# Partial sums of a layer's first two chunks in five stretches instead of two, their weight loads placed by the modulation's progress

## The chip, the cores and the metric

The kernel runs on one core of one Trainium2 chip. The metric is the device time of one execution in microseconds; the median of a few runs counts.

## The reference

The reference is a two-layer diffusion backbone. Each layer modulates its normalised input, projects it through one wide matrix, and runs two token mixers on the parts (differential attention and a gated MLP) before an output projection. What matters here is how a layer begins:

```python
mod = silu_c @ w_ada[layer] + b_ada[layer]                 # 2048 -> 3 x 2048
shift, scale, gate = [m[:, None, :] for m in jnp.split(mod, 3, axis=-1)]
hn = _rmsnorm(h, norm_g) * (1.0 + scale) + shift           # 256 latent + 256 context tokens
z = hn @ w_in                                              # 2048 -> 11264
q, k, v, ga, ub, vb, gb, mg = jnp.split(z, cuts, axis=-1)
```

Each feature of `hn` needs its own columns of `w_ada`, and each column of `z` contracts over all 2048 features, 16 tiles of 128. All is float32; the kernel splits every operand of the large products into a high and a low float32r part and multiplies three times (high by high, high by low, low by high).

## The kernel before

Every engine gets its instructions in the order in which a planner (`Builder`) writes them. The planner keeps an estimate of the time on each engine and interleaves a stream of weight products on PE with side work written as generators. What it writes is fixed in the built program: at run time each engine goes through its list in order and waits on semaphores.

**Pieces.** Weights come from memory in pieces of 512 KB in the order of a list, `plan`. SP issues all their loads, in that order, into four buffers named `raw`. There are two kinds. A piece of `w_in` holds two feature tiles by 512 columns; ACT casts it into `wh`, DVE subtracts to get `wl` (line 47 is the helper through which all work on DVE, ACT and POOL is issued), and then its `raw` buffer is free. A piece of `w_ada` for layer 0 holds four feature tiles by 256 columns (`ada4_segs`) and is read by PE as it lies in `raw`; its buffer is free when PE has used it. Below, A1 to A64 are these 64 pieces of layer 0's modulation in order; on PE each is four matmuls `ms<-raw,s` (eight in the profile, two passes each).

**Modulation.** Layer 0's shift and scale are made in eight groups of two feature tiles; a group is eight pieces, four for the shift and four for the scale (`ada_pe`). After each four, ACT copies the row and PE turns it into columns (`ms<-c,w`, the column matmuls); after eight, `x_trans` transposes the two feature tiles of the tokens (`ms<-c,s`, four per tile), DVE applies scale and shift, and ACT and DVE split the result into the operand `x`. So feature tiles 2g and 2g+1 can be multiplied only after group g.

**The first two chunks.** X (queries and keys of the first pair of heads) and Y (the first 512 columns of v) are products of 512 tokens by 512 columns over the 16 feature tiles. A *step* is one token tile by one feature tile: three matmuls of 512 columns, `mm<-wh,x`, `mm<-wl,x`, `mm<-wh,x`. A piece of `w_in` makes eight steps, both chunks 128. There are four PSUM banks `mm`, as many as one chunk has token tiles. X's first half (tiles 0 to 7) is accumulated, copied by ACT into an SBUF tile (`keep`), then Y's first half, then the second halves, whose sums DVE adds to the parked ones (`drop`, `from_psum`). A table `quota` says how many steps stand before each modulation piece: none before the first 14, one before each of the next 26, two before each of the last 24, 74 in all; the remaining 54 follow. The pieces of `w_in` stand in the plan one place ahead of A14, A22, A30, A38, A43 and so on. The look-ahead of the loads (`loads`) is six pieces, as far as `raw` buffers are free.

Of the kernel before, what the change touches and what calls it, by code (L numbers as in the profile page):

```python
# [38 lines left out]
class Engine:  # L39
    """An engine whose instructions run in the order in which they are written."""  # L40

# [12 lines left out]
class Builder:  # L54
    """Interleaves the stream of weight matmuls with everything else. Side work is written as
    generators; a yield waits for what the generator has issued and may ask for buffers."""

# [25 lines left out]

# [1 line left out]
    def t(self, tag, shape, dt=F32):  # L85
# [19 lines left out]

# [1 line left out]
    def account(self, key, name, kw):  # L107
# [35 lines left out]

# [1 line left out]
    def spawn(self, gen, urgent=False, front=False):  # L145
# [33 lines left out]
    def loads(self):  # L179
        while self.nraw < min(self.at + 6, len(self.plan)) and len(self.pool["raw"]) > self.spare:  # L180
            self.grab("raw", 1, 1e18)
            i = self.nraw
            self.nraw += 1
            if i in self.extra:
                self.extra[i]()
            self.ready[i] = Event()
            self.spawn(self.split(i), urgent=True)
# [34 lines left out]

# [1 line left out]
    def matmul(self, out, lhsT, rhs, start, stop, slow=1.0):  # L224
# [20 lines left out]

# [1 line left out]
    def hl(self, h, l, src):  # L247
# [15 lines left out]

# [1 line left out]
    def load(self, segs, kt):  # L265
# [29 lines left out]
    def piece(self, segs, kt):  # L295
# [6 lines left out]
        return self.ready.pop(i).hl  # L302

    def piece_done(self, tag="wh"):
        self.pool[tag].append(self.now)

    def tok_steps(self, ps, xh, xl, segs, tiles, k0, k1, nk=KT, first=0, on_tile=None, pre=None, front=False):
        """out[tokens of a tile, columns] += x[tokens, k] w[k, columns]"""
        for kt in range(k0, k1, 2):
            if pre is not None:  # L310
                pre(kt)
            h, l = self.piece(segs, kt)
            for t, c0, c1 in tiles:
                if t not in ps:
                    self.take("mm")
                    ps[t] = self.bank("mm")
                for k in range(2):
                    ts = slice(t * P, (t + 1) * P)
                    self.mm3(ps[t][:, c0:c1], xh(kt + k)[:, ts], xl(kt + k)[:, ts],
                             h[:, k, c0:c1], l[:, k, c0:c1], kt + k == first, kt + k == nk - 1)  # L320
                    if kt + k == nk - 1 and on_tile is not None:
                        self.spawn(on_tile(t, ps.pop(t)), front=front)
                    yield
            self.piece_done()
# [8 lines left out]
    def col_chunk(self, xh, xl, segs, ntok, nk=KT, on_tile=None):  # L333
        """out[columns of a tile, tokens] += w[k, columns] x[tokens, k]"""
        ps = {}
        for kt in range(0, nk, 2):
            h, l = self.piece(segs, kt)
            for ct in range(4):
                if ct not in ps:
                    self.take("mm")  # L340
                    ps[ct] = self.bank("mm")
                for k in range(2):
                    cs = slice(ct * P, (ct + 1) * P)
                    self.mm3(ps[ct][:, :ntok], h[:, k, cs], l[:, k, cs],
                             xh(kt + k)[:, :ntok], xl(kt + k)[:, :ntok], kt + k == 0, kt + k == nk - 1)
# [9 lines left out]
def dit_kernel(ctx, tc, x, c, ctxt, c_ctx, w_ada, b_ada, norm_g, w_in, q_norm_g, k_norm_g,  # L355
# [4 lines left out]
    V, A = B.V, B.A  # L360

# [1 line left out]
    crow = B.w2()  # L363
# [121 lines left out]

# [1 line left out]
    def qk_segs(L, p):  # L487
# [15 lines left out]
    GK = KT // NG  # L503
    LEAD = 1
    START, RISE = 14, 40
    quota = [0] * START + [1] * (RISE - START) + [2] * (8 * NG - RISE)
    begin = [next(i for i in range(8 * NG) if sum(quota[:i + 1]) > 8 * n) for n in range((sum(quota) + 7) // 8)]
    first = [(segs, k, k + 2, k0) for k0 in (0, 8) for segs in (qk_segs(0, 0), in_segs(0, VO)) for k in range(k0, k0 + 8, 2)]

    for L in range(DEPTH):  # L510
        if L == 0:
            for i in range(8 * NG):
                for n, at_ in enumerate(begin):
                    if max(at_ - LEAD, 0) == i:
                        B.add(*first[n][:3])
                B.whole.add(len(B.plan))
                B.add(ada4_segs(0, (i // 4 % 2) * D + i // 8 * 256), 4 * (i % 4), 4 * (i % 4) + 4, 4)
            for segs, k0, k1, _ in first[len(begin):]:
                B.add(segs, k0, k1)
        else:  # L520
            B.add(in_segs(L, VO), 0, KT)
            B.add(qk_segs(L, 0), 0, KT)
            B.add(in_segs(L, VO), 0, KT)
# [13 lines left out]

# [1 line left out]
    mod_ev = {}  # L539
# [22 lines left out]
    def ada_pe(L, grp, work):  # L562
        for which, c0 in (("shift", 0), ("scale", D)):
# [3 lines left out]
            for kt in range(0, KT, 4):  # L567
                for _ in range(quota[8 * grp + (4 if which == "scale" else 0) + kt // 4]):
                    next(work, None)
                    B.tick()  # L570
                w, _ = B.piece(ada4_segs(L, c0 + grp * 256), kt)
# [105 lines left out]
    def x_trans2(L, xt, xth, xtl, kt, s, ev, cond):  # L677
        """two feature tiles of one of the two streams"""
        yield dict(pe=1, ms=1, cond=cond)
# [19 lines left out]

# [1 line left out]
    xn_ev = [Event() for _ in range(4)]  # L701
# [31 lines left out]
    def layer(L, xt, xn_ev, x_in=None):  # L733
# [5 lines left out]

# [1 line left out]
        qk_tiles = [(t, 0 if t in qt else 256, 512) for t in full]  # L741
# [87 lines left out]

# [1 line left out]
        dn = [None, None]  # L831
# [140 lines left out]

# [1 line left out]
        if x_in is None:  # L974
# [8 lines left out]
        if L == 0:  # L983
            parts = {}

            def keep(name):
                def on_tile(t, ps):
# [4 lines left out]
                    else:  # L992
                        yield dict(cond=lambda: parts[name] is not None)
                    A.copy(out=parts[name][:, t], in_=ps)
                    B.rel("mm")
                return on_tile

            all_tiles = [(t, 0, 512) for t in full]

            def drop(name, gen, n={"X": 0, "Y": 0}):  # L1000
                yield from gen
                n[name] += 1
                if n[name] == 4:
                    B.rel("s8")

            def first_steps():
                ps_ = {}
                for segs, k0, k1, h0 in first:
                    name = "X" if segs == qk_segs(0, 0) else "Y"
                    if h0 == 0:  # L1010
                        on_tile = keep(name)
                    elif name == "X":
                        on_tile = lambda t, ps: drop("X", qk_first(st0, t, ps, parts["X"][:, t]))
                    else:
                        on_tile = lambda t, ps: drop("Y", v_first(v0, t, ps, parts["Y"][:, t]))
                    yield from B.tok_steps(ps_, xh, xl, segs, all_tiles, k0, k1, h0 + 8, h0, on_tile,
                                           lambda kt: [B.wait_ev(xev[k]) for k in (kt, kt + 1)])

            work = first_steps()
            for grp in range(NG):  # L1020
# [8 lines left out]
                if grp == 0:  # L1029
                    B.spawn(rope_tables(65000.0))  # L1030
            for _ in work:
                B.tick()
# [8 lines left out]

# [1 line left out]
        spawn_pair(st0, v0, 0)  # L1043
# [7 lines left out]

# [1 line left out]
        class Operand:  # L1053
            """[feature, token] operand of a branch's projection, in halves of four feature tiles"""

# [185 lines left out]

# [1 line left out]
        gates = {}  # L1243
# [107 lines left out]

# [1 line left out]
        mh, ml = m_op  # L1353
# [113 lines left out]
```

## Time and profile before

| | |
|---|---|
| median of 3 runs | 2330.43 us (2327.11 to 2331.57) |
| span of the profiled execution, first to last instruction | 2330.1 us |
| the profiled execution's own time | not recorded apart from its span |
| PE busy | 2290.1 us, 98% of the span |
| DVE, ACT busy | 1488.3 us (64%), 883.2 us (38%) |
| DMA | 384.18 MB, 165 GB/s in the mean |

The kernel stands almost wholly on PE. PE's idle time is therefore what there is to win or lose, together with the stretches in which its clock is granted at 1.2 instead of 2.4 GHz. The first 160 us are a stage of their own: DMA is busy there nine tenths of the time and moves 46 MB, most of it `w_ada`.

### The profile page before, as it was taken

Reading aid. Unit: us, or ns where it says so; the run is one execution under the profiler, and the core shown is the slowest. Engines: PE = TensorE matmul, PEld = TensorE weight load, DVE = VectorE, ACT = ScalarE, POOL = GpSimd, SP = SyncE. Lnnn points to the kernel's source line nnn. Section 1 sums busy time; section 2 is a strip of 40 time slices with the busy share of each in tenths; the row PEclk is TensorE's granted clock in tenths of the full one; section 3 lists DMA queues with packets and bytes.
Section 4 is the critical chain, followed back from the end, with each engine's and each line's share of the span. In section 5 each row is a group of like instructions: output and inputs, shape, how many; then the busy total and the mean of one; then the engine's idle time right before and its main releaser. Section 6 shows DMA issues by size and latency. Waiting matters only on the chain.

```text
span 2330.1 us, 28951 instructions
## 1 busy us (share of the span) xinstructions
PE 2290.1 (98%) x11018; PEld 1844.9 (79%) x11018; DVE 1488.3 (64%) x2353; ACT 883.2 (38%) x1395; POOL 111.9 (5%) x119
## 2 busy tenths in 40 slices
PE   6899999999999999999999999999999999999999
PEld 2467877878888888878888888888888888888887
DVE  3346675665436665587766776776757766667655
ACT  3234445453332122222222322545535554444443
POOL 2000110110000000000000000001101100000000
PEclk9999999999999999999999999999999999999999
DMA  9872222223334555555555565654324567777765
GB/s 309 272 241 82 82 73 73 86 82 113 100 91 145 172 156 154 162 172 169 175 156 162 156 220 179 193 165 136 106 91 131 172 184 249 249 252 249 257 200 181
DMA packets 229628, 384.18 MB, mean 165 GB/s; under 512 B 13423, under 2 KB 79057, under 8 KB 228721
## 3 DMA queue, kind: packets, MB, share of 16 engines
q1 hardware_dynamic: 227616, 377.55, 52.3%
q0 software_dynamic: 1872, 4.78, 1.0%
q8 instruction: 86, 1.41, 0.3%
q14 instruction: 54, 0.43, 0.1%
HBM read 377.04 MB, written 5.24 MB: 164 GB/s over the span
## 4 chain that ended last, share of the span: by engine, by line
PE 94%; DMA 3%; DVE 2%; ACT 0%; issue 0%; POOL 0%; POOLq 0%; DVEq 0%; ACTq 0%
PE mm L225 86%; PE ms L225 5%; PE ms L232 3%; DMA raw<-in_w_ada_dram 2%; DVE wl L47 1%; DMA raw<-in_w_in_dram 0%; DVE w L47 0%; DVE ws L47 0%; DMA w<-in_k_norm_g_dram 0%; DVE s L47 0%; ACT w L47 0%; DVE x L47 0%; POOL w L397 0%; ACT wh L47 0%; ACT s L47 0%
## 5 line engine op out<-in xcount | busy, mean ns | idle before, releaser
L225 PE MATMUL mm<-wh,x 128*128 128x512 f32 (+1 forms) x4352 | 1387.5, 390 | 1.3 <-DVE w L47 1.0
L225 PEld LDWEIGHTS mm<-wh,x 128*128 128x128 f32 x4352 | 811.1, 188 | 189.4 <-issue 30.0
L47 DVE TENSOR_TENSOR wl<-raw,wh 128x1024 fp32r<-128x1024 f32 x496 | 606.6, 1223 | 471.7 <-ACT wh L47 470.4
L47 ACT CAST wh<-raw 128x1024 fp32r<-128x1024 f32 x496 | 522.4, 1054 | 923.8 <-PE mm L225 668.8
L225 PE MATMUL mm<-wl,x 128*128 128x512 f32 (+1 forms) x2176 | 836.5, 384 | 1.4 <-DVE wl L47 1.4
L225 PEld LDWEIGHTS mm<-wl,x 128*128 128x128 f32 x2176 | 410.4, 189 | 73.7 <-DVE wl L47 2.8
L225 PE MATMUL mm<-x,wh 128*128 128x512 f32 x1024 | 316.3, 390 | 0.0
L47 DVE SCALAR_TENSOR_TENSOR ws<-raw,c,ws 128x512 f32<-128x512 f32 x420 | 288.1, 748 | 12.7 <-DMA raw<-in_w_ada_dram 11.8
L225 PEld LDWEIGHTS mm<-x,wh 128*128 128x128 f32 x1024 | 191.7, 188 | 39.6
L225 PE MATMUL mm<-x,wl 128*128 128x512 f32 x512 | 199.3, 389 | 0.0
L225 PE MATMUL mm<-s,wh 128*128 128x512 f32 x512 | 157.7, 389 | 0.0
L47 POOL TENSOR_TENSOR st<-st,c 128x8 f32<-128x8 f32 (+3 forms) x76 | 90.5, 1198 | 893.3 <-DVE st L47 886.4
L225 PEld LDWEIGHTS mm<-x,wl 128*128 128x128 f32 x512 | 96.1, 188 | 20.4
L225 PEld LDWEIGHTS mm<-s,wh 128*128 128x128 f32 x512 | 96.1, 188 | 19.9
L225 PE MATMUL mm<-s,wl 128*128 128x512 f32 x256 | 99.7, 389 | 0.9 <-DVE wl L47 0.9
L225 PE MATMUL mm<-wh,s 128*128 128x512 f32 x256 | 81.7, 391 | 0.0
L47 ACT ACTIVATE w<-mm 128x512 f32<-128x512 f32 x72 | 42.9, 599 | 99.1 <-PE mm L225 99.1
L47 ACT ACTIVATE w<-ms,st 128x512 f32<-128x512 f32 (+1 forms) x96 | 58.7, 617 | 50.4 <-DVE st L47 50.4
L232 PE MATMUL ms<-c,w 128*128 128x128 f32 (+1 forms) x434 | 69.6, 273 | 7.4 <-DVE w L47 6.5
L47 DVE TENSOR_REDUCE st<-ms 128x1 f32<-128x512 f32 (+1 forms) x96 | 54.5, 597 | 31.1 <-PE ms L225 31.1
L232 PEld LDWEIGHTS ms<-c,w 128*128 128x128 f32 (+1 forms) x434 | 53.2, 140 | 26.4 <-issue 6.9
L225 PE MATMUL ms<-raw,s 128*32 128x256 f32 x512 | 48.2, 453 | 18.7 <-DMA raw<-in_w_ada_dram 17.9
(116 smaller groups left out, 1373.2 us busy)
## 6 DMA issues: line engine op xcount, KB each, us to landing
raw<-in_w_in_dram SPq DMA_DIRECT2D x296, 512.0 KB, 3.9
raw<-in_w_ada_dram SPq DMA_DIRECT2D x192, 512.0 KB, 4.7
raw<-in_w_out_dram SPq DMA_DIRECT2D x72, 512.0 KB, 4.4
raw<-in_w_in_dram SPq DMA_DIRECT2D x128, 256.0 KB, 3.1
raw<-in_w_proj_b_dram SPq DMA_DIRECT2D x32, 512.0 KB, 4.5
raw<-in_w_proj_a_dram SPq DMA_DIRECT2D x32, 512.0 KB, 4.6
s<-in_ctx_dram SPq DMA_DIRECT2D x2, 1024.0 KB, 10.8
s<-in_x_dram SPq DMA_DIRECT2D x2, 1024.0 KB, 12.7
```

Source lines behind the costliest of these rows:

```text
L47: ins = getattr(self.eng, name)(**kw)
L225: self.tc.keep_in_program_order(self.nc.tensor.matmul(out=out, lhsT=lhsT, rhs=rhs, start=start, stop=stop))
L232: self.tc.keep_in_program_order(self.nc.tensor.transpose(out=out, in_=in_, identity=identity))
```

## The change

X and Y now run in five stretches of the contraction, tiles 0-1, 2-3, 4-7, 8-11 and 12-15, with X's part of each stretch ahead of Y's. The first stretch's sums are copied by ACT into the parked tile as before; those of the next three are added to it by DVE; the last is added as the old second half was. The weight pieces stand in the plan at places worked out by `place`: 10, 14, 18, 22, 26, 34, 34, 38, 42, 50, 50, 54, 58, 66, 66, 70, each ahead of the modulation piece of that number counted from 0. The table of steps is gone. `work` is called before each modulation piece: it owes two steps more each time (at most eight), and writes steps as long as the planner thinks that the next one's input and weights are there, and either steps are owed or the modulation piece has not landed by the planner's estimate. The look-ahead is nine pieces. The rest of the diff removes comments.

```diff
-        while self.nraw < min(self.at + 6, len(self.plan)) and len(self.pool["raw"]) > self.spare:
+        while self.nraw < min(self.at + 9, len(self.plan)) and len(self.pool["raw"]) > self.spare:
...
-    LEAD = 1
-    START, RISE = 14, 40
-    quota = [0] * START + [1] * (RISE - START) + [2] * (8 * NG - RISE)
...
-    first = [(segs, k, k + 2, k0) for k0 in (0, 8) for segs in (qk_segs(0, 0), in_segs(0, VO)) for k in range(k0, k0 + 8, 2)]
+    STRETCHES = ((0, 2), (2, 4), (4, 8), (8, 12), (12, 16))
+    FIRST, PACE = 10, 4
+    first = [(segs, k, k + 2, n) for n, (k0, k1) in enumerate(STRETCHES)
+             for segs in (qk_segs(0, 0), in_segs(0, VO)) for k in range(k0, k1, 2)]
+    place = [max(FIRST + PACE * n, 8 * (f[1] // GK + 1) + 2) for n, f in enumerate(first)]
...
-                for _ in range(quota[8 * grp + (4 if which == "scale" else 0) + kt // 4]):
-                    next(work, None)
-                    B.tick()
+                work(2, ada4_segs(L, c0 + grp * 256), kt)
...
-                        yield dict(cond=lambda: parts[name] is not None)
-                    A.copy(out=parts[name][:, t], in_=ps)
+                        yield dict(cond=lambda: parts[name] is not None and kept[name, t] == n)
+                    if n == 0:
+                        A.copy(out=parts[name][:, t], in_=ps)
+                    else:
+                        V.tensor_tensor(out=parts[name][:, t], in0=ps, in1=parts[name][:, t], op=ALU.add)
...
+            def work(n, segs, kt):
+
+
+                gone["due"] = min(gone["due"] + n, 8)
+                while True:
+                    here = B.landed(segs, kt)
+                    if can() and (gone["due"] > 0 or not here):
+                        next(steps, None)
+                        gone["steps"] += 1
+                        gone["due"] -= 1
+                        B.tick()
+                    elif here:
+                        return
+                    else:
+                        B.wait(lambda: can() or B.landed(segs, kt))
```

PE has 10144 rows of instructions before and after. Ahead of A64 stand 74 steps before and 100 after. On PE around A19, before: A18 (`raw_330`), the column matmuls, one step, A19, the transposes of one tile, and the next step:

```order
L225 MATMUL ms_351<-raw_330,s_12_93 32x256 x4
L225 MATMUL ms_374<-c_97,w_93_356 128x2 x2
L225 MATMUL mm_383<-wh_313,x_27_119 128x512
L225 MATMUL mm_383<-wl_314,x_27_119 128x512
L225 MATMUL mm_383<-wh_313,x_28_120 128x512
L225 MATMUL ms_351<-raw_340,s_12_93 32x256 x4
L232 MATMUL ms_393<-c_73,s_2_69 128x128
...
L225 MATMUL mm_383<-wh_313,x_27_119 128x512
L225 MATMUL mm_383<-wl_314,x_27_119 128x512
```

After, from A18 (`raw_369`) on: A19, the transposes of a tile, A20, the transposes of the other, A21, A22, the column matmuls, and then the first of eight steps in a row ahead of A23:

```order
L225 MATMUL ms_406<-raw_369,s_12_93 32x256 x4
L225 MATMUL ms_406<-raw_399,s_12_93 32x256 x4
L232 MATMUL ms_458<-c_73,s_2_69 128x128
...
L225 MATMUL ms_406<-raw_424,s_12_93 32x256 x4
L232 MATMUL ms_472<-c_73,s_2_69 128x128
...
L225 MATMUL ms_481<-raw_448,s_12_93 32x256 x4
L225 MATMUL ms_481<-raw_450,s_12_93 32x256 x4
L225 MATMUL ms_499<-c_97,w_119_482 128x2 x2
L225 MATMUL mm_506<-wh_421,x_27_119 128x512
```

The steps that stood one by one between the pieces stand together now: none from A18 to A22, eight before A23. In the same way there are none from A27 to A31, A33 to A34, and A50 to A52, and eight, six and eight (one and seven around column matmuls) before A33, A36 and A54; the first eight stand before A14.

On SP, the loads ahead of A38 before: A36 and A37, one piece of `w_in`, A38, A39:

```order
L269 DMA raw_616<-in_w_ada_dram 128x4x256
L269 DMA raw_628<-in_w_ada_dram 128x4x256
L269 DMA raw_637<-in_w_in_dram 128x2x256 x2
L269 DMA raw_663<-in_w_ada_dram 128x4x256
L269 DMA raw_678<-in_w_ada_dram 128x4x256
```

After, A32 to A34, two pieces of `w_in`, A35 (`raw_780`) and A36:

```order
L269 DMA raw_666<-in_w_ada_dram 128x4x256
L269 DMA raw_677<-in_w_ada_dram 128x4x256
L269 DMA raw_692<-in_w_ada_dram 128x4x256
L269 DMA raw_716<-in_w_in_dram 128x2x256 x2
L269 DMA raw_719<-in_w_in_dram 128x2x512
L269 DMA raw_780<-in_w_ada_dram 128x4x256
L269 DMA raw_787<-in_w_ada_dram 128x4x256
```

Two weight pieces stand side by side now, between A34 and A35, and on PE the eight steps before A33 come ahead of all three. The first weight piece of all stands between A10 and A11 on SP's list, before between A13 and A14.

On PE at the end of the modulation, before, from the last column matmuls on (`wh_1222` is the piece of tiles 12 and 13; six more of its steps follow the last transposes, then the first step of tile 14):

```order
L225 MATMUL ms_1253<-c_97,w_254_1230 128x2 x2
L225 MATMUL mm_1199<-wh_1169,x_27_119 128x512
...
L225 MATMUL mm_1139<-wh_1222,x_27_119 128x512
L225 MATMUL mm_1139<-wl_1223,x_27_119 128x512
L225 MATMUL mm_1139<-wh_1222,x_28_120 128x512
L232 MATMUL ms_1271<-c_73,s_2_69 128x128
...
L225 MATMUL mm_1139<-wh_1222,x_27_119 128x512
...
L232 MATMUL ms_1283<-c_73,s_2_69 128x128
```

After, the last four steps of tiles 12 and 13 (the fourth is shown), the column matmuls, both tiles' transposes, and then the first step of tile 14 (`wh_1347` is the piece of tiles 14 and 15):

```order
L225 MATMUL mm_1387<-wh_1227,x_28_120 128x512
L225 MATMUL ms_1400<-c_97,w_289_1381 128x2 x2
L232 MATMUL ms_1413<-c_73,s_2_69 128x128
...
L232 MATMUL ms_1421<-c_73,s_2_69 128x128
...
L225 MATMUL mm_1340<-wh_1347,x_27_119 128x512
L225 MATMUL mm_1340<-wl_1348,x_27_119 128x512
```

The steps that stood between the last columns and the first use of the last two tiles stand ahead of the columns now.

## Rows read from the trace of the kernel before

**Rows 1.** The page, part 1: busy us of each engine (share of the span).

```profile
PE 2290.1 (98%) x11018; PEld 1844.9 (79%) x11018; DVE 1488.3 (64%) x2353; ACT 883.2 (38%) x1395; POOL 111.9 (5%) x119
```

**Rows 2.** Windows: us; PE, PEld, DVE, ACT, POOL busy; granted clock; DMA share; GB/s.

```profile
0.00:37.00 37.00, 18.46 (x126) 6.83 (x126) 11.62 (x34) 15.22 (x39) 11.71 (x27) 1.00 0.97 329
37.00:156.00 119.00, 108.27 (x734) 61.50 (x735) 41.20 (x122) 26.92 (x44) 1.07 (x2) 0.94 0.89 273
156.00:300.00 144.00, 144.00 (x712) 114.74 (x711) 98.78 (x205) 62.73 (x137) 16.77 (x12) 1.00 0.30 92
300.00:2330.10 2030.10, 2019.37 (x9451) 1661.82 (x9449) 1336.73 (x1994) 778.31 (x1177) 82.34 (x78) 1.00 0.52 161
```

**Rows 3.** Waits of PE, 37 to 156 us: total us, times, longest us.

```profile
PE ms L225 <- DMA raw<-in_w_ada_dram: 10.5, 10, 3.5
PE mm L225 <- DVE wl L47: 0.2, 1, 0.2
```

**Rows 4.** Timeline of PE: three pieces that it waited for.

```profile
40.56 1.08 PE L225 MATMUL ms<-raw,s 128*32 128x256 f32 x8 [3.35 <-DMA raw<-in_w_ada_dram]
...
65.53 0.64 PE L225 MATMUL ms<-raw,s 128*32 128x256 f32 x8 [3.54 <-DMA raw<-in_w_ada_dram]
...
83.51 0.64 PE L225 MATMUL ms<-raw,s 128*32 128x256 f32 x8 [0.52 <-DMA raw<-in_w_ada_dram]
```

**Rows 5.** Windows around the two long waits, columns as in rows 2.

```profile
37.00:40.56 3.56, 0.21 (x2) 0.12 (x2) 2.01 (x5) 1.05 (x1) 0.00 (x0) 0.84 0.97 258
40.56:47.00 6.44, 6.44 (x32) 2.70 (x33) 0.00 (x0) 0.32 (x1) 0.00 (x0) 0.56 0.88 291
47.00:62.00 15.00, 13.94 (x107) 7.13 (x105) 5.53 (x15) 2.90 (x6) 1.07 (x2) 1.00 0.91 238
66.00:74.00 8.00, 8.00 (x40) 4.68 (x37) 1.71 (x7) 0.21 (x1) 0.00 (x0) 0.57 0.76 238
74.00:90.00 16.00, 14.31 (x112) 6.97 (x111) 7.46 (x37) 2.73 (x6) 0.00 (x0) 1.00 0.90 279
```

**Rows 6.** Timeline of PE: a piece and two steps, A64, and dense steps.

```profile
106.59 0.64 PE L225 MATMUL ms<-raw,s 128*32 128x256 f32 x8
107.16 0.50 PE L225 MATMUL mm<-wh,x 128*128 128x512 f32 x1
...
108.74 0.64 PE L225 MATMUL ms<-raw,s 128*32 128x256 f32 x8
...
154.06 0.64 PE L225 MATMUL ms<-raw,s 128*32 128x256 f32 x8
...
163.43 0.62 PE L225 MATMUL mm<-wh,x 128*128 128x512 f32 x2
...
164.11 0.62 PE L225 MATMUL mm<-wh,x 128*128 128x512 f32 x2
```

**Rows 7.** Timeline of PE: two pieces in a row, each waited for.

```profile
30.29 1.08 PE L225 MATMUL ms<-raw,s 128*32 128x256 f32 x8 [0.33 <-DMA raw<-in_w_ada_dram]
31.80 0.65 PE L225 MATMUL ms<-raw,s 128*32 128x256 f32 x4 [0.43 <-DMA raw<-in_w_ada_dram]
```

**Rows 8.** The loads into `raw` from 37 to 156 us.

```profile
DMA to landing us min/median/max: 3.6/5.0/9.1
```

**Rows 9.** Timeline of DVE after the last columns; its additions from PSUM, 130 to 260 us.

```profile
160.27 0.15 DVE L47 COPY st<-ms 128x4 f32<-128x4 f32 x1
...
162.11 1.22 DVE L47 TENSOR_TENSOR wl<-raw,wh 128x1024 fp32r<-128x1024 f32 x1
...
164.14 1.47 DVE L47 TENSOR_TENSOR x<-w,x 128x512 fp32r<-128x512 f32 x2
...
L47 DVE TENSOR_TENSOR w<-mm,s 128x512 f32<-128x512 f32 x8 | 5.4, 685 | 0.5 <-PE mm L225 0.4
```

**Rows 10.** Waits of PE from 160 us to the end.

```profile
PE mm L225 <- DVE wl L47: 2.0, 3, 0.9
PE ms L232 <- DVE s L47: 1.3, 1, 1.3
```

More of the change, by code (lines that the diff above doesn't have):

```diff
@@ L302, in piece, with landed @@
         return self.ready.pop(i).hl
+    def landed(self, segs, kt):
+        i = next((i for i in range(self.at, self.at + 12) if i not in self.taken and i < len(self.plan)
+                  and self.plan[i] == (segs, kt)), None)
+        return i in self.ready and self.ready[i].at is not None and self.ready[i].at <= self.now
     def piece_done(self, tag="wh"):
@@ L503, in dit_kernel @@
     GK = KT // NG
-    LEAD = 1
-    START, RISE = 14, 40
-    quota = [0] * START + [1] * (RISE - START) + [2] * (8 * NG - RISE)
-    begin = [next(i for i in range(8 * NG) if sum(quota[:i + 1]) > 8 * n) for n in range((sum(quota) + 7) // 8)]
-    first = [(segs, k, k + 2, k0) for k0 in (0, 8) for segs in (qk_segs(0, 0), in_segs(0, VO)) for k in range(k0, k0 + 8, 2)]
+    STRETCHES = ((0, 2), (2, 4), (4, 8), (8, 12), (12, 16))
[3 more added lines that the diff above has]
+    place = [max(FIRST + PACE * n, 8 * (f[1] // GK + 1) + 2) for n, f in enumerate(first)]
     for L in range(DEPTH):
@@ L512, in dit_kernel @@
             for i in range(8 * NG):
-                for n, at_ in enumerate(begin):
-                    if max(at_ - LEAD, 0) == i:
+                for n, at_ in enumerate(place):
+                    if at_ == i:
                         B.add(*first[n][:3])
@@ L517, in dit_kernel @@
                 B.add(ada4_segs(0, (i // 4 % 2) * D + i // 8 * 256), 4 * (i % 4), 4 * (i % 4) + 4, 4)
-            for segs, k0, k1, _ in first[len(begin):]:
-                B.add(segs, k0, k1)
+            for n, at_ in enumerate(place):
+                if at_ >= 8 * NG:
+                    B.add(*first[n][:3])
         else:
@@ L984, in layer, with keep @@
             parts = {}
-            def keep(name):
+            kept = {(name, t): 0 for name in "XY" for t in full}
+            def keep(name, n):
                 def on_tile(t, ps):
@@ L992, in on_tile, with drop @@
                     else:
-                        yield dict(cond=lambda: parts[name] is not None)
-                    A.copy(out=parts[name][:, t], in_=ps)
+                        yield dict(cond=lambda: parts[name] is not None and kept[name, t] == n)
[3 more added lines that the diff above has]
+                        V.tensor_tensor(out=parts[name][:, t], in0=ps, in1=parts[name][:, t], op=ALU.add)
                     B.rel("mm")
+                    kept[name, t] += 1
                 return on_tile
             all_tiles = [(t, 0, 512) for t in full]
-            def drop(name, gen, n={"X": 0, "Y": 0}):
-                yield from gen
+            def drop(name, t, make, n={"X": 0, "Y": 0}):
+                yield dict(cond=lambda: kept[name, t] == len(STRETCHES) - 1)
+                yield from make()
                 n[name] += 1
@@ L1007, in first_steps, with can @@
                 ps_ = {}
-                for segs, k0, k1, h0 in first:
+                for segs, k0, k1, n in first:
                     name = "X" if segs == qk_segs(0, 0) else "Y"
-                    if h0 == 0:
-                        on_tile = keep(name)
+                    if n < len(STRETCHES) - 1:
+                        on_tile = keep(name, n)
                     elif name == "X":
-                        on_tile = lambda t, ps: drop("X", qk_first(st0, t, ps, parts["X"][:, t]))
+                        on_tile = lambda t, ps: drop("X", t, lambda: qk_first(st0, t, ps, parts["X"][:, t]))
                     else:
[L1015 to L1019, printed above, removed]
+                        on_tile = lambda t, ps: drop("Y", t, lambda: v_first(v0, t, ps, parts["Y"][:, t]))
+                    yield from B.tok_steps(ps_, xh, xl, segs, all_tiles, k0, k1, STRETCHES[n][1], STRETCHES[n][0],
+                                           on_tile, lambda kt: [B.wait_ev(xev[k]) for k in (kt, kt + 1)])
+            steps = first_steps()
+            gone = dict(steps=0, due=0)
+            def can():
+                if gone["steps"] >= 8 * len(first):
+                    return False
+                segs, k, _, _ = first[gone["steps"] // 8]
+                return (all(xev[k + a].at is not None and xev[k + a].at <= B.now for a in range(2))
+                        and (gone["steps"] % 8 != 0 or B.landed(segs, k)))
+            def work(n, segs, kt):
[11 more added lines that the diff above has]
+                        B.wait(lambda: can() or B.landed(segs, kt))
             for grp in range(NG):
@@ L1030, in layer @@
                     B.spawn(rope_tables(65000.0))
-            for _ in work:
+            for _ in steps:
                 B.tick()
```

## The prediction

> **What bounds the kernel now.** I read the page first: PE is busy 2290.1 of 2330.1 us, so all that an edit can win is the 40.0 us in which PE stands still, and the stretches in which it runs at half its clock [rows 1, 2]. Windows over the span say where those are: 18.5 us lie before 37 us, 10.7 between 37 and 156 us, none from 156 to 300, 10.7 in all the rest [rows 2]. Before 37 us there is no transposed input yet and PE waits for the first loads; neither kernel can fill that. The change works in the second stretch, where the modulation's 64 pieces (A1 to A64) pass through PE with chunk steps between them. There the list of waits names one cause: ten waits for `w_ada` pieces, 10.5 us [rows 3]; two of them are long, 3.35 us ahead of 40.56 and 3.54 us ahead of 65.53 [rows 4]. DMA is busy 0.89 of that stretch and PE 0.91 [rows 2], so the two are nearly balanced, and what decides is how evenly PE gives buffers back.
>
> The clock follows those two waits. Granted clock is 0.84 and 0.56 from 37 to 47 us and 0.57 from 66 to 74 us, and 1.00 between and after [rows 5]: twice 6.8 us at 1.2 instead of 2.4 GHz (twice the missing share, times the length). Of the first, 5.7 us fall on work (2.8 us lost), of the second all (3.4 us). Waits of half a microsecond, as at 83.51 [rows 4], left the clock at 1.00.
>
> **What the change moves, in order.** The matmuls are the same in number and size on PE; the time can differ only by waits, clock, and switching between kinds. A step (three matmuls) takes 0.68 us in a dense run, and A plus two steps 2.15 us; with A at 0.57 that is 2.15 - 0.57 - 1.36 = 0.22 us for each run of steps between pieces [rows 6].
>
> *Saved.* Before A64 the steps stand in 53 runs in the old order and 43 in the new: 10 x 0.22 = 2.2 us. The waits of before go: 10.5 us. The slow stretch at 66 us goes: 3.4 us. The one at 40 us I keep, since in both orders PE comes out of thin work there. Together -16.1 us.
>
> *Added.* In the new order 100 steps stand before A64 instead of 74, but not evenly: a run of eight (seven and one around a column matmul) before A14, eight before A23, eight before A33, six before A36, eight before A54; and ahead of these bursts runs of pieces with nothing between them but transposes and column matmuls: A18 to A22, A27 to A32, A33 to A35, A49 to A53. The reason is in the input: feature tiles 2g and 2g+1 can't be multiplied before group g's modulation is through. There are four raw buffers, and a modulation piece gives its buffer back only when PE has used it. A burst of eight steps is 5.4 us in which PE returns none; at 1.5 us a piece (30.29 to 31.80 [rows 7]) DMA could land 3.6. Then the pieces are eaten at 0.57 us each, and PE waits for DMA, which needs 3.6 us at least and 5.0 in the median from issue to landing [rows 8]. I reckon with 4.0, near the short end, since these queues start empty. By place:
> (a) X's first piece now lies ahead of A11 in SP's queue, so the pieces after it land one place later: 1.5 us.
> (b) A21's buffer comes free with A18, 4.0 us before it lands; under that lie two pieces and eight transposes, 1.9 us: 2.1. The rope table's two loads on POOL's queue fall there too (before, they stood ahead of A25's 3.54 us wait; I take 1.5), and A22 is 0.9 late: 4.5 us, bounds 2 to 6.5.
> (c) A28 to A32 come at 1.5 us and are used in 0.57: four times 0.9 less transposes: 3.0 us, bounds 1.5 to 4.5.
> (d) While the eight steps before A33 run, A33, A34 and two weight pieces hold the four buffers, so A35 is issued when A33 is done: 4.0 - 0.57 - 0.2 = 3.2 us, bounds 2 to 5.
> (e) A51 is issued with A49's end, under A50, a column matmul and eight transposes (about 2.1 us): 1.9, and A52 and A53 0.8 each: 3.5 us, bounds 2 to 5.
> (f) The last transposes. Before, two steps, one and six lay, with the transposes, between the last column matmuls and the first step of tile 14; now nothing but the transposes does, 0.7 us. The old chain from the column copy to the last x ran on DVE from 160.27 to 165.61 us, 5.3 us, a weight split of 1.22 in its midst [rows 9]; x of tile 14 is there about 0.7 sooner, 4.7 us after the columns. 4.7 - 0.7: 4.0 us, bounds 2.8 (no split in the midst) and 6 (one more ahead, as before).
> (g) X's end and Y's end were 32 steps apart, now 16, so queries and keys have 11 us of cover instead of 22 for DVE's chain. PE's waits for DVE after 160 us were single ones of at most 1.3 us [rows 10]; I take 1.5, bounds 0 to 4.
> Sum of waits: 21.2 us.
>
> *Clock.* Both waits over 3 us in the old trace were followed by 6.8 us at 1.2 GHz, and here a burst of full work follows each, so a fall costs 3.4 us. Six places can bring one: b to g. I take b, d, e and f, where a wait of about 2 us or more stands: 13.6 us; bounds none and six (20.4).
> The Trainium skill speaks against such bursts: "TensorE: Matmul & The Clock Gate", section "HAM oscillation — how this bites in real kernels", says that where a group of matmuls is followed by a wait for the next load, every group starts on the slow clock. The two long waits of this trace agree with it [rows 4, 5]; what it would make of the time is a rival below.
>
> *Costed at nothing.* The parked sums: 24 additions from PSUM on DVE at 0.685 us, the length of the same addition now [rows 9], 16.4 us on an engine that is busy 41.2 of 119 us there [rows 2]. They lie beside PE's steps: a tile's bank is asked for again six steps, 4.1 us, after its last matmul. With that cover gone, each of eight stretch starts would pay about 1 us. The look-ahead of nine instead of six: four raw buffers bound it in both, and SP's order is the same from the modulation's end on, so nothing behind moves; the 10.7 us of idle time past 300 us stay.
>
> Sum: -16.1 + 21.2 + 13.6 = +18.7 us on the profiled execution's 2330.1, 2348.8; its span stands 0.3 us under the median of the runs, 2330.43, so the time forecast is **2349 us**.
>
> **Rivals.**
> *Clock holds.* The gaps inside the runs of pieces are short, about 0.9 us, and at 83.51 such a gap did not lower the clock [rows 4, 5]. Against it: in b, d and e a whole wait of 2 to 4 us follows thin work. Without the 13.6 us: +5.1, 2335. A chance of 0.15; half of it within 0.2% of before, half slower.
> *Bursts hidden (not slower).* DMA fills four buffers during each burst, 3.6 pieces of time, so that a run of up to four pieces finds all landed. The point that decides is the run's length against four: the runs are 5, 6, 3 (with two weight pieces in the same buffers) and 5, all past it. If it held all the same, then c, d and e and most of b go; a, the rope loads' 1.5, f and g stay, 8.5 us, with one slow stretch after f: -16.1 + 8.5 + 3.4 = -4.2, 2326, or 2321 if f's wait is hidden as well. A chance of 0.14.
> *Every burst starts slow.* c falls too, thin work for nine microseconds ahead of eight steps: five times 3.4 us, 17.0 instead of 13.6, 2352. For it speaks that nothing in this trace shows PE keep 2.4 GHz through work that thin; against it, that no wait inside c is over 0.9 us. This is the page's rule just named, worked out here from [rows 5]. A chance of 0.15.
> *Banks.* ACT and DVE work in order: a parking addition queued behind a weight split waits for that split's load, and PE's next stretch for the bank. Before, `PE mm <- DVE wl` in this stretch is one wait of 0.2 us [rows 3], which speaks against it. Eight starts at 1 us: +8 more, 2357. A chance of 0.12.
> *Nothing moves.* The order shows that it does; 0.02 for the effects cancelling.
>
> **Numbers.** The forecast has 0.42, with its own range of 2340 to 2358 from the bounds of b to g and of the number of slow stretches. For 8 in 10 the range must take in the held clock (2335) and the banks (2357): 2332 to 2359; it leaves out the hidden bursts, 0.14, and some of the tails. What differs by under 0.2%, 4.7 us, can hardly be told from no change. Faster: two thirds of the hidden bursts, 0.09, and a tail, 0.10. Same: their other third, half of the held clock, and 0.02: 0.14 less the tails, 0.13. Slower: the rest, 0.77.
>
> **What would show it.** In the new trace: waits of PE for `w_ada` between 37 and 185 us of some 16 us in place of 10.5, the longest ahead of A21, A35 and A51; granted clock at 1.2 GHz in four or more stretches before 220 us; A64 near 180 us with 100 steps done, where before it stood at 154.06 with 74 [rows 6]; a wait of 3 to 6 us at the first step of tile 14, named by DVE; windows past 300 us as before. I would be wrong if the waits for `w_ada` fell below 7 us (the bursts are hidden), if the clock held at 1.00 from 50 us on, or if PE's share of 37 to 156 us rose over 0.95.

## The result and the profile after

The changed kernel takes 2351.2 us (2349.5 to 2352.44), the kernel before 2329.02 us beside it: a ratio of 1.0093, 95% interval 1.0078 to 1.0107. It is slower by 22.2 us; the profiled executions differ by 19.6 (span 2349.7 against 2330.1). The forecast was 2349.

I read the new trace in the order of the prediction. First PE's busy time, part 1 of the page (as [rows 1]), and windows over the span (as [rows 2]; us, then busy us of PE, PEld, DVE, ACT and POOL, granted clock, DMA share, GB/s).

```profile
PE 2298.9 (98%) x11018; PEld 1852.9 (79%) x11018; DVE 1502.5 (64%) x2377; ACT 882.1 (38%) x1395; POOL 113.0 (5%) x119
```

```profile
0.00:37.00 37.00, 17.75 (x114) 6.13 (x114) 12.53 (x34) 15.34 (x38) 11.80 (x27) 1.00 0.97 323
37.00:156.00 119.00, 101.46 (x635) 63.69 (x633) 47.36 (x122) 26.25 (x42) 1.06 (x2) 0.87 0.76 236
156.00:185.00 29.00, 29.00 (x175) 18.79 (x175) 11.88 (x27) 4.25 (x7) 0.00 (x0) 0.94 0.69 214
185.00:220.00 35.00, 31.03 (x146) 23.98 (x145) 29.42 (x62) 13.72 (x25) 7.88 (x4) 0.95 0.38 121
300.00:2349.70 2049.70, 2039.62 (x9549) 1677.66 (x9547) 1347.65 (x2016) 784.96 (x1196) 82.39 (x79) 1.00 0.52 160
```

PE stands still for 50.8 us (2349.7 - 2298.9) instead of 40.0: 17.5 between 37 and 156 us where it was 10.7, 4.0 between 156 and 300 where it was nothing, 10.1 after 300 where it was 10.7. So 10.8 of the 19.6 us are waits; the other 8.8 are longer busy time for the same matmuls. DMA's share from 37 to 156 us fell from 0.89 to 0.76: in the first three or four us of a burst it fills the four buffers, then it stands empty until PE gives one back, and PE waits for it afterwards. So it is in the second half of the eight steps before A33:

```profile
100.00:104.00 4.00, 4.00 (x30) 2.96 (x32) 2.79 (x9) 1.31 (x2) 0.00 (x0) 1.00 0.00 0
```

The waits of PE from 37 to 156 us (as [rows 3]) and the timeline of PE where it waited (start us, length us; in brackets the wait ahead and what ended it):

```profile
PE ms L225 <- DMA raw<-in_w_ada_dram: 17.5, 12, 5.4
```

```profile
35.94 1.08 PE L225 MATMUL ms<-raw,s 128*32 128x256 f32 x8 [0.81 <-DMA raw<-in_w_ada_dram]
37.47 1.08 PE L225 MATMUL ms<-raw,s 128*32 128x256 f32 x8 [0.45 <-DMA raw<-in_w_ada_dram]
...
59.09 0.64 PE L225 MATMUL ms<-raw,s 128*32 128x256 f32 x8 [1.42 <-DMA raw<-in_w_ada_dram]
65.73 1.08 PE L225 MATMUL ms<-raw,s 128*32 128x256 f32 x8 [5.42 <-DMA raw<-in_w_ada_dram]
67.12 1.08 PE L225 MATMUL ms<-raw,s 128*32 128x256 f32 x8 [0.30 <-DMA raw<-in_w_ada_dram]
89.05 0.64 PE L225 MATMUL ms<-raw,s 128*32 128x256 f32 x8 [0.66 <-DMA raw<-in_w_ada_dram]
90.43 0.64 PE L225 MATMUL ms<-raw,s 128*32 128x256 f32 x8 [0.74 <-DMA raw<-in_w_ada_dram]
92.00 1.08 PE L225 MATMUL ms<-raw,s 128*32 128x256 f32 x8 [0.38 <-DMA raw<-in_w_ada_dram]
93.91 1.08 PE L225 MATMUL ms<-raw,s 128*32 128x256 f32 x8 [0.82 <-DMA raw<-in_w_ada_dram]
107.81 0.64 PE L225 MATMUL ms<-raw,s 128*32 128x256 f32 x8 [3.20 <-DMA raw<-in_w_ada_dram]
148.94 0.64 PE L225 MATMUL ms<-raw,s 128*32 128x256 f32 x8 [2.29 <-DMA raw<-in_w_ada_dram]
150.99 1.08 PE L225 MATMUL ms<-raw,s 128*32 128x256 f32 x8 [1.40 <-DMA raw<-in_w_ada_dram]
152.51 1.08 PE L225 MATMUL ms<-raw,s 128*32 128x256 f32 x8 [0.44 <-DMA raw<-in_w_ada_dram]
...
193.28 0.50 PE L225 MATMUL mm<-wh,x 128*128 128x512 f32 x1 [2.72 <-ACT x L47]
```

These are A12, A13, A20 to A22, A29 to A32, A35, A51 to A53 and the first step of tile 14, the places (a) to (f) of the prediction. None of the waits of [rows 4] is left.

Windows of PE laid on the stretches where the granted clock was half (us, PE busy, clock, DMA share, GB/s), with the four us ahead of the first and of the second, and one over the first steps:

```profile
60.70:74.40 13.70, 8.37 (x33) 0.50 0.72 206
91.50:98.30 6.80, 5.60 (x25) 0.50 1.02 337
108.50:111.90 3.40, 3.40 (x9) 0.50 1.04 349
149.50:159.70 10.20, 8.36 (x37) 0.50 0.79 256
193.80:197.30 3.50, 3.40 (x9) 0.51 0.32 104
56.70:60.70 4.00, 2.19 (x24) 1.00 0.81 153
87.50:91.50 4.00, 2.59 (x31) 0.99 0.97 323
...
39.00:43.40 4.40, 4.40 (x14) 1.00 1.04 360
```

Five stretches at 1.2 GHz hold 29.1 us of work, half of which, 14.6 us, is lost. The first begins at 60.7 us, 0.4 us into the long wait for A21: the fall came after the thin work ahead of that wait, with one wait of 1.42 us in it. Another lies before the first of them and the clock's column does not show it: from 39 to 43.4 us it says 1.00, but the matmuls start 0.43 us apart, where dense ones start 0.23 apart [rows 6]:

```profile
39.07 0.63 PE L225 MATMUL mm<-wl,x 128*128 128x512 f32 x1
39.50 0.63 PE L225 MATMUL mm<-wh,x 128*128 128x512 f32 x1
```

That loses 2.2 us more. Together 16.8 us against 6.3 before [rows 5]: 10.5 us more. The busy time grew by 8.8, which is 1.7 less.

### The profile page after: what moved, and what is told of

It is laid out like the page before. It is cut to its first block, busy times and chain, and to the rows that moved or that the text cites. A ratio compares the mean times of both kernels' runs of the same rounds, so it can differ in the third digit from the quotient of the medians.

```text
span 2349.7 us, 28968 instructions
## 1 busy us (share of the span) xinstructions
PE 2298.9 (98%) x11018; PEld 1852.9 (79%) x11018; DVE 1502.5 (64%) x2377; ACT 882.1 (38%) x1395; POOL 113.0 (5%) x119
## 4 chain that ended last, share of the span: by engine, by line
PE 94%; DMA 3%; DVE 2%; ACT 0%; issue 0%; POOL 0%; SPq 0%; ACTq 0%; DVEq 0%
PE mm L225 86%; PE ms L225 5%; PE ms L232 3%; DMA raw<-in_w_ada_dram 2%; DVE w L47 1%; DVE wl L47 1%; DVE s L47 0%; DVE ws L47 0%; ACT w L47 0%; POOL st L47 0%; DVE x L47 0%; ACT wh L47 0%; DMA raw<-in_w_in_dram 0%; DVE st L47 0%; SPq L269 0%
## 5 line engine op out<-in xcount | busy, mean ns | idle before, releaser
L225 PEld LDWEIGHTS mm<-x,wl 128*128 128x128 f32 x512 | 96.1, 188 | 20.4
## 6 DMA issues: line engine op xcount, KB each, us to landing
s<-in_ctx_dram SPq DMA_DIRECT2D x2, 1024.0 KB, 10.8
```

The costliest lines, as they stand in the source:

```text
L225: self.tc.keep_in_program_order(self.nc.tensor.matmul(out=out, lhsT=lhsT, rhs=rhs, start=start, stop=stop))
```

## The experiments

Times are medians, beside the kernel before in the same series; ratios are to it, with 95% intervals. "After" means the changed kernel. My theory is called the pacing theory below: bursts of steps and runs of bare pieces make PE wait for `w_ada`, and the clock falls at those places.

**One: the look-ahead alone undone.**

```diff
-        while self.nraw < min(self.at + 9, len(self.plan)) and len(self.pool["raw"]) > self.spare:
+        while self.nraw < min(self.at + 6, len(self.plan)) and len(self.pool["raw"]) > self.spare:
```

> The changed kernel with the look-ahead of six pieces again, all else as changed. Pacing theory (the loss comes from bursts of steps with runs of bare pieces between them, by waits for w_ada and the slow stretches after these): four raw buffers bound the loads in both, so 2351 us, within 3 us. Rival, the longer look-ahead brings the waits: nearer to 2329, at least 5 us under 2351.

2354.45 us, ratio 1.0099 (1.0082 to 1.0116), after 1.0093. Waits for `w_ada` from 37 to 156 us are as long as after:

```profile
PE ms L225 <- DMA raw<-in_w_ada_dram: 17.9, 14, 5.2
```

The look-ahead neither brought the loss nor hides it.

**Two and three: the old table of steps in five stretches, and in four.**

```diff
+    quota = [0] * 14 + [1] * 26 + [2] * 24
+    begin = [next((i for i in range(8 * NG) if sum(quota[:i + 1]) > 8 * n), 8 * NG) for n in range(len(first))]
+    place = [b - 1 if b < 8 * NG else b for b in begin]
...
-                gone["due"] = min(gone["due"] + n, 8)
-                while True:
...
+                for _ in range(quota[gone["piece"]]):
+                    next(steps, None)
+                    B.tick()
+                gone["piece"] += 1
```

The run with four stretches has this too, and `STRETCHES = ((0, 2), (2, 4), (4, 8), (8, 16))`.

> The changed kernel, five stretches and parked sums included, with the steps placed by the old table (none before the first 14 pieces, one before each of 26, two before each of 24) and each weight piece one place ahead of its first step. Pacing theory: waits for w_ada from 37 to 156 us return to about 10.5 us, clock stretches as before, A64 near 154 us; queries and keys end 16 steps before v instead of 32, which may cost 1 to 4 us: 2330 to 2335. Rival, the parked sums or the banks cost: it stays at 2340 or above, and PE's waits in this stage name DVE or ACT.

> The run with the old table, with four stretches (the last from tile 8 to 15) instead of five: X's and Y's sums end 32 steps apart as before, not 16; 16 parking additions fewer by eight. Theory that the nearness of the two ends is what the old table's run lost: from the issue of the 41st to the 61st weight piece it took 86.9 us against 81.8 before; here 82 again, no wait of 1 us for the queries' and keys' chain around 190 us, and 3 to 5 us less than that run: 2332 to 2335. Rival, parking itself costs: it stays at 2336 to 2339.

Five stretches: 2337.69 us, ratio 1.0027 (1.0016 to 1.0037). Four: 2331.26 us, 1.0003 (0.9994 to 1.0012). So more than two thirds of the loss goes with the old places of steps and weight pieces, and the rest with the fifth stretch. PE's waits with five stretches, from 37 to 156 us and, in part, after 156 us:

```profile
PE ms L225 <- DMA raw<-in_w_ada_dram: 7.0, 6, 2.6
...
PE ms L232 <- DVE w L47: 3.2, 3, 1.5
PE mm L225 <- DVE w L47: 2.3, 3, 1.0
```

The same with four stretches:

```profile
PE ms L225 <- DMA raw<-in_w_ada_dram: 10.0, 6, 4.1
...
PE mm L225 <- DVE w L47: 1.0, 1, 1.0
PE ms L232 <- DVE w L47: 0.6, 1, 0.6
```

With five stretches all waits after 156 us sum to 9.8 us, with four to 5.0, before to 5.7. X and Y end 16 steps apart instead of 32, and PE's rows name DVE, whose chain makes the queries and keys; I take this for the prediction's (g), at 4 to 6 us with the old table. The fifth stretch also brings eight more parking additions, and no run tells the two apart. Parking as such costs nothing that can be measured: the run with four stretches has 16 parking additions and takes the time of before. My 2330 to 2335 for five stretches was too low by the fifth stretch's part.

**Four and five: dummy matmuls in the waits.** They have a piece's shape and write columns of the modulation's bank that nobody reads. They take no part in the planner's times, so that the order of all else is the same.

```diff
+    FILL = {20: 8, 21: 30, 29: 4, 30: 4, 31: 2, 32: 5, 35: 18, 51: 13, 52: 8, 53: 2}
...
                 work(2, ada4_segs(L, c0 + grp * 256), kt)
+                for _ in range(FILL.get(8 * grp + (4 if which == "scale" else 0) + kt // 4 + 1, 0)):
+                    tc.keep_in_program_order(nc.tensor.matmul(out=prow[0:32, 256:512], lhsT=cpk[:, 0],
+                                             rhs=cpk.rearrange("p k c -> p (k c)")[:, 0:256], start=kt == 0, stop=kt == 0))
```

The second of the two runs has `{20: 2, 21: 9, 29: 1, 30: 1, 32: 1, 35: 6, 51: 4, 52: 2}`.

> The changed kernel with dummy matmuls of a piece's own shape (0.14 us each, into columns of the modulation's bank that nobody reads) ahead of the ten pieces that PE waited for, four fifths of each wait; the order of all else is the same and nothing is left out. Theory that the clock is a cost of its own, set by what PE did before: the slow stretches at 60, 92, 109 and 150 us go, with about 22 us of busy time at half clock in them, so 11 us less: 2340. Rival, the pieces set the pace there anyway, so that a faster PE only waits more: 2349 to 2352. Rival, the clock falls whatever PE does in the waits: 2351 with the stretches still there.

> The filler of the run before cost 0.43 us for each dummy matmul, not 0.14, so that it overran the waits three times over; here 26 of them, 11.2 us in all, within eight of the waits (17 us). The order of all else is the same and nothing is left out. Theory that the slow clock is a cost of its own: the stretches at 60, 92, 109 and 150 us go, with 12.8 us lost in them; a faster PE meets later pieces earlier, so some comes back as waits: 2340 to 2345. Rival, the pieces set the pace and the clock costs nothing: 2350 or above, with waits for w_ada longer by what the clock gave.

The first took 2361.68 us, ratio 1.0131 (1.0116 to 1.0147), 10 us more than after: I had mis-sized it. The timeline of PE in it shows 59 of the 60 passes of the 30 dummies ahead of A21:

```profile
60.63 12.92 PE L580 MATMUL ms<-s 128*32 128x256 f32 x59
```

They take 0.43 us each, three times what I had taken from a piece, and stand for 12.9 us where the wait was 5.4. It still shows that the clock follows PE's own work: no stretch at half clock is left before 200 us, though steps and bare pieces stand as after. The second, sized by that, took 2343.9 us, ratio 1.0057 (1.0042 to 1.0072): 7 to 8 us less than after by the medians (4.6 us by the profiled executions, of which this one is the slowest of its four), with nothing taken out. Its windows of PE:

```profile
37.00:67.20 30.20, 27.53 (x167) 1.00 0.80 228
67.20:74.00 6.80, 6.80 (x22) 0.50 0.53 169
74.00:186.60 112.60, 104.59 (x709) 1.00 0.79 249
```

The stretches at 91, 108 and 149 us are gone, the one at 60 is shorter by half; the one behind the first step of tile 14, where no dummies stand, is still there, and longer (187 to 193 us). Its waits for `w_ada` are 9.2 us and the dummies 11.2, together 20.4 where after has 17.5: about 3 us of what the clock gave came back as waits. So the slow clock is a cost of its own, not something that the pieces' pace hides.

**Six: the rope table's loads, in the changed kernel.**

```diff
-                    B.spawn(rope_tables(65000.0))
+                    B.spawn(rope_tables(115000.0))
```

> The changed kernel with the rope table's two small loads on POOL's queue and their work on DVE planned later (115 instead of 65 in the planner's clock). If these loads hold up the longest wait (5.42 us ahead of 65.73): that wait falls to 2 to 3 us, what the burst alone makes by the prediction's (b), and the time by 3 to 5 us, to 2347. If the burst makes all of it: the wait stays above 4 us and the time at 2351.

2349.48 us, ratio 1.0082 (1.0067 to 1.0097), not distinguishable from after. The timeline of PE at A21, at A31 to A34 in one row, and at A35:

```profile
62.72 0.64 PE L225 MATMUL ms<-raw,s 128*32 128x256 f32 x8 [2.51 <-DVE x L47]
...
93.81 1.93 PE L225 MATMUL ms<-raw,s 128*32 128x256 f32 x32
...
103.32 1.08 PE L225 MATMUL ms<-raw,s 128*32 128x256 f32 x8 [6.11 <-DMA raw<-in_w_ada_dram]
```

The longest wait falls from 5.42 to 2.51 us: 2.9 of it were the two small loads; 2.5 are left to the run of bare pieces from A18 on. (The row names DVE; the piece landed 0.1 us ahead of its first matmul, so it is the load that ended this wait.) A21's load took 5.7 us from issue to landing here and 8.9 us in the changed kernel. The DMA engines were as busy with the small loads as without, but moved half as much; from 58 to 62 us, first in the changed kernel, then in this run:

```profile
58.00:62.00 4.00, 1.23 (x12) 0.58 (x12) 2.29 (x5) 1.61 (x3) 0.00 (x0) 0.84 1.00 162
```

```profile
58.00:62.00 4.00, 1.22 (x12) 0.58 (x12) 2.50 (x6) 1.61 (x3) 0.00 (x0) 1.00 1.00 323
```

What was won was given back at A35, 6.11 us instead of 3.20. But there the order is no longer the same: with the tables later, the planner put the eight steps ahead of A31 instead of A33, so that A31 to A34 stand bare between them and A35. A35's load went out right behind three loads of `w_in` and took 7.3 us to land instead of 3.8. So this run shows the price of the small loads at A21, where the order up to there is the same, and not what they are worth in the whole.

**Seven: the same edit in the kernel before; eight: with the first step one piece earlier too** (`quota = [0] * 13 + [1] * 27 + [2] * 24`).

> The kernel before with the rope table's two small loads planned later, as in the run with late tables. If these loads make the 3.54 us wait ahead of 65.53: it falls below 1 us, the slow stretch of 6.8 us behind it goes, and the time falls by 5 to 7 us, to 2322 to 2325. If the pieces are late there without them, or the wait comes back further on as it did in the changed kernel: 2327 to 2331.

> The kernel before with late tables, and its first step one modulation piece earlier (none before the first 13 pieces, one before each of 27, two before each of 24: 75 steps before A64). Theory that the long wait at 40 us is a lack of work there: it falls from 3.1 to about 2 us and its slow stretch shortens, 1 to 2 us under the run with late tables alone: 2324 to 2325. Rival, the weight piece, one place earlier too, delays the pieces by as much: 2326 to 2328.

The first: 2325.8 us, ratio 0.9983 (0.9973 to 0.9992), faster than both kernels and between the two ranges that I had given. The waits of its PE from 37 to 156 us:

```profile
PE ms L225 <- DMA raw<-in_w_ada_dram: 9.6, 9, 3.1
```

and the window of PE there:

```profile
37.00:156.00 119.00, 108.96 (x759) 0.99 0.91 285
```

The waits' sum hardly moved (10.5 before); what went is the long one ahead of 65.53 and the clock's fall behind it. The mean clock is 0.99 where it was 0.94. Of the 5 us, 3.4 are that stretch; 1.7 are the stretch at 40 us, which is half as long here as before [rows 5]:

```profile
40.30:43.80 3.50, 3.46 (x20) 1.24 (x20) 0.00 (x0) 0.00 (x0) 0.00 (x0) 0.53 0.69 223
```

The loads that were moved stood at 56 us, so this part may be chance. The second: 2329.41 us, ratio 0.9991 (0.9982 to 1.0000), above both ranges that I had given. The wait at 40 us is shorter and stands at 37.61, but others came. The timeline of its PE:

```profile
37.61 0.64 PE L225 MATMUL ms<-raw,s 128*32 128x256 f32 x8 [2.03 <-DMA raw<-in_w_ada_dram]
...
93.68 0.64 PE L225 MATMUL ms<-raw,s 128*32 128x256 f32 x8 [2.30 <-DMA raw<-in_w_ada_dram]
```

**Nine to eleven: how many steps may be owed.**

```diff
-                gone["due"] = min(gone["due"] + n, 8)
+                gone["due"] = min(gone["due"] + n, 2)
```

The others have 4, and 2 with the late tables of six.

> The changed kernel with the steps owed limited to two instead of eight: no eight steps in a row; two before each piece from A14 to A29, 96 steps before A64 instead of 100. Five stretches, parked sums, places and look-ahead as changed. Pacing theory: the waits for w_ada from 37 to 156 us fall from 17 to under 10 us, and the slow stretches there from 34 us to under 14; the end of the modulation and the nearness of X's and Y's ends keep their 4 to 6 us: 2335 to 2342. Rival, bursts don't matter and it is the stretches themselves or the number of steps: 2347 or above.

> The changed kernel with at most four steps owed, between the change (eight: 2351) and the run that owes two (2335): bursts of four before A14, A23 and A33. Pacing theory: waits and slow stretches grow with the burst, from 8.9 us of waits for w_ada (two) to 17.1 (eight): 2337 to 2343. Rival, any run of bare pieces costs the whole: 2347 or above.

> At most two steps owed, with late tables: the evened change without the small loads on POOL's queue at 56 us. The wait of 2.28 us ahead of 66.51 falls or goes; as the loads gave 5 us in the kernel before, where a slow stretch hung on the wait, and no slow stretch hangs on it here, 2 us: 2331 to 2334. Rival, they give as much as there, 5 us: 2329 to 2331. Rival, the loads only hit other pieces later on: 2335.

Eight owed (after) 2351 us, four 2341.08 (ratio 1.0048, 1.0033 to 1.0064), two 2335.31 (1.0018, 1.0009 to 1.0028), two with late tables 2335.36 (1.0024, 1.0012 to 1.0036). Waits for `w_ada` from 37 to 156 us with four owed, and with two:

```profile
PE ms L225 <- DMA raw<-in_w_ada_dram: 11.4, 8, 2.9
```

```profile
PE ms L225 <- DMA raw<-in_w_ada_dram: 8.9, 9, 2.3
```

The window of PE from 37 to 156 us with two owed, where the clock's mean was 0.87 after:

```profile
37.00:156.00 119.00, 110.56 (x739) 1.00 0.85 267
```

The column flatters it: up to 45 us matmuls start 0.43 us apart here too, under a column of 1.00, as they do up to 43.4 us in the changed kernel:

```profile
40.55 0.63 PE L225 MATMUL mm<-wl,x 128*128 128x512 f32 x1
40.98 0.63 PE L225 MATMUL mm<-wh,x 128*128 128x512 f32 x1
```

What is gone are the four stretches from 60 to 160 us. One constant takes back four fifths of the loss (4.6 us are left of 22), with five stretches, parked sums, places and look-ahead as in the change. PE stands still for 3.7 us between 156 and 300 us in this run, where before it does not, in waits for ACT and DVE around the first step of tile 14 and at 200 us, so most of what is left is the prediction's (f) and (g). Late tables add nothing to it, which is the side of the last rival: no slow stretch hung on the wait that they shorten, other waits take it over (8.6 us in all), and one slow stretch is new (83 to 86 us).

**Twelve: a mix** of four stretches, an even table (`[0] * 11 + [2, 2, 1] + [1] * 26 + [2] * 18 + [1] * 6`, weight pieces two places ahead) and late tables.

> A mix: four stretches (tiles 0-1, 2-3, 4-7, 8-15), so that X's and Y's ends lie 32 steps apart again; steps by a table: two before A12 and A13, one before each of A14 to A40, two before A41 to A58, one before the last six, 73 before A64; weight pieces two places ahead of their first step; look-ahead nine; late tables. Pacing theory: the waits at 40 and 65 us of the kernel before go with their slow stretches, the last transposes keep their cover: 2318 to 2324. Rival, the parked sums or the places cost what the waits give: 2328 to 2334.

2330.99 us, ratio 1.0001 (0.9991 to 1.0010): the rival's side. The waits are shorter and more, and their sum is that of before:

```profile
PE ms L225 <- DMA raw<-in_w_ada_dram: 10.4, 12, 1.8
```

## Why the prediction was right, step by step

The sum said waits +10.7 (21.2 added, 10.5 saved), clock +10.2 (13.6 added, 3.4 saved), switching -2.2: +18.7. The rows say waits +10.8, clock +10.5, and -1.7 for the rest, which fits the switching but was not measured by itself: +19.6. (Counted from 37 us instead of 39, where PE's work is at half rate too, the clock's part is 0.8 larger and the rest -2.5.) The mechanism held: waits behind bursts and bare runs, and slow stretches with them, in about equal parts. Such closeness of the sum is partly luck; by places it is less good:

| place | predicted us | wait in the rows |
|---|---|---|
| a, before A14 | 1.5 | 1.26 |
| b, A20 to A22 | 4.5 (2 to 6.5) | 7.14 |
| c, A29 to A32 | 3.0 (1.5 to 4.5) | 2.60 |
| d, A35 | 3.2 (2 to 5) | 3.20 |
| e, A51 to A53 | 3.5 (2 to 5) | 4.13 |
| f, first step of tile 14 | 4.0 (2.8 to 6) | 2.72 |
| g, X's and Y's ends | 1.5 (0 to 4) | 1.1 |

- *b was mis-sized*, past its upper bound. The rope loads were priced at 1.5 us; run six measured 2.9. Without them b is 4.4 (1.18, 2.51 and 0.68) where the sum had 3.0: it took 4.0 us from issue to landing for A21, and in run six it was 5.7. For A35 the 4.0 held (3.8).
- *f was too long*, and 2.72 lies just under its lower bound: x of tile 14 comes 4.2 us after the column matmuls began at 189.12, of which the transposes and columns cover 1.4; the row names ACT, whose cast is the last step of that chain, and not DVE as I had expected.
- *g* is one wait for DVE of 1.1 us at 218.65 us; before has none between 156 and 300 us. Later waits fell by 0.7, so that all waits for DVE after 156 us sum to 6.1 against 5.7. The fifth stretch cost 4 to 6 us with the old table (runs two and three).
- *Which stretches are slow* I had wrong at c, and right at b for a reason that does not hold. I had b, d, e and f fall, where a wait of about 2 us or more stands, and c hold, since no wait in c is over 0.9 us. c fell: in the four us ahead of 91.5 PE was busy for 2.59 of 4.00, with no wait over 0.74. And at b the clock fell 0.4 us after the long wait began; in the four us ahead PE was busy for 2.19 of 4.00. Several short waits with short pieces between did what one long wait did at A35. That is the rival of the bursts that start slow. The Trainium skill's "TensorE: Matmul & The Clock Gate", section "HAM oscillation — how this bites in real kernels", tells of every group of matmuls that starts slow behind a wait longer than the group. At c the pieces of 0.57 us stand behind waits of 0.38 to 0.82 us, which is close to that pattern; but in the page's own case each wait brings the fall by itself, and here none did.
- *The size of the clock's term* came out by luck: five falls instead of four, of 4.2, 2.8, 1.7, 4.2 and 1.7 us instead of 3.4 each, since the stretches were 13.7, 6.8, 3.4, 10.2 and 3.5 us long.
- *The first slow stretch kept*: right in time (2.2 us after, 2.8 before), though the clock's column shows it only before. After, nothing fell there: the piece at 37.47 us already took 1.08 us, so PE had not risen yet.
- *A64 near 180 us* was 185.66, late by what b's wait (2.6 us) and c's slow stretch (2.8 us) added to the forecast.
- *Rivals.* Hidden bursts would have shown waits under 7 us: 17.5. The held clock would have left 1.00 after 50 us: four stretches from 60 to 160. Banks: no wait of PE from 37 to 156 us names DVE or ACT, and run three has none of the loss with parking in it. The 2321 of the hidden bursts does not come out of its terms: without f's 4.0 us the sum gives 2322, and 2319 without the slow stretch behind f too.

What stays open: the -1.7 us, and why the fifth stretch costs about 5 us with the old table and one wait of 1.1 us after; I did not follow DVE's order there. The cover of the last transposes was not restored by itself; runs two and three have it, and there the wait of 2.72 us is gone.

## What to carry to other kernels

Where two streams share four buffers and DMA is nearly as busy as PE, an even mix mattered more than how much work stands early: 100 steps ahead of A64 in bursts lost to 74 spread singly, and limiting the debt from eight steps to two took back four fifths. Once there are no bursts, an edit mostly moves the waits about (6.7 to 10.5 us in the eight kernels without them, and the one with least is not the fastest); what can be won is that no stretch of them, long or made of several short ones, takes the clock down, since here the clock cost as much as the waits. Before pricing a run of loads, ask what else moves meanwhile: half of the longest wait came from two small loads on another queue.

## What the runs showed of the hardware

- A piece's four matmuls, each for its own 32 partitions of the output, take 0.57 us together [rows 6]; a matmul of that shape repeated on one group of 32 takes 0.43 us each time (run four), both with the clock's column at 1.00. Side by side they run three times as fast. The Trainium skill's "TensorEngine Tiling (Array Packing)", section "Theoretical Speedup", gives up to four times for a dimension of 32 or less, and this trace stays below it.
- The clock's column can say 1.00 while matmuls run at half rate, as from 39 to 43.4 us after and up to 45 us with two steps owed; the spacing of equal matmuls (0.43 against 0.23 us) is the safer reading at the start of a trace.
- Two loads of 32 KB on POOL's queue held up a 512 KB piece on SP's queue by 2.9 us (run six), where pieces in a row land 1.5 us apart [rows 7]. Meanwhile the DMA engines were 1.00 busy and moved 162 GB/s, against 323 without these loads.
